# Expert weights in 2 MB pieces of 16 KB runs for pairs of experts, and a next-to-last piece in two parts

## The chip, the cores and the metric

The kernel runs on one core of a Trainium2 chip. The metric is the device time of one execution in microseconds. Before the change the median of three runs is 1400.31 us (1399.62 to 1402.27).

## The reference, cut to what matters

One layer for 256 tokens of width 1024, in float32. A mixer with four branches (RWKV7, HGRN2, mLSTM, RG-LRU) is followed by a layer norm, a mixture of 32 experts with the best four for each token, a gated projection called PLE, and a second layer norm:

```python
mix = merged @ w_out[layer]                      # merged: the four gated branches
x = _layernorm(DEEPNORM_ALPHA * x + mix, ln1_g[layer], ln1_b[layer], dt)
moe_out = moe(x.reshape(bsz * seq, D_MODEL), router_w[layer], ...)
ple = jax.nn.sigmoid(x @ ple_gate_w[layer]) * (p[layer] @ ple_proj_w[layer])
x = _layernorm(DEEPNORM_ALPHA * x + moe_out + ple, ln2_g[layer], ln2_b[layer], dt)
```

An expert takes its tokens through a product of 1024 x 2048 (`w_gu`, a gate half and an up half of 1024 columns each), a clamped SwiGLU, and a product of 1024 x 1024 (`w_dn`). The weights of 32 experts are 403 MB in float32, and each is used once.

## The kernel before, in words

Phase 1 (to about 435 us) computes the four branches, the merge, the first layer norm and the router. Its products are made of three passes each (lines 378 to 380) on operands that ACT and DVE split into a high and a low part (lines 373 and 374). Phase 2 is the expert stage. Experts go in 16 pairs; the first expert of a pair uses partitions 0 to 63 of a PSUM bank, the second 64 to 127.

All weights come through one list, `stream`, filled by `want` in the order of use. Before, an entry is one 1 MB piece of one expert: 512 rows by 512 columns, laid out in HBM as 128 runs of 8,192 bytes, one for each partition (`chunks`, line 2117). The two experts of a pair alternate in the list. For one pair, `want_up` (line 1392) lists four column blocks x two row halves x two experts, and `want_down` (line 1399) two x two x two. For two of the pairs (`PLE`) it also lists half of `w_pg` in two pieces, and half of `w_pp` (512 KB).

`pump` (line 311) walks the list as far as there are buffers, and issues each transfer on SP's queue. There are two kinds of buffers. The 14 slots (`NSLOT`, line 202) hold 8 KB on each partition. The rest is the `Arena` (line 128), from which all other tiles come as well; its allocator likes to keep whole blocks of 2,048 float columns free (`B`), and `ar.blocks()` counts those. `st["keep"]` is a reserve of buffers that the stream leaves for other tiles once `st["slots"]` is 0, which is the case in the expert stage. `drop` (line 368) gives a piece's buffer back; from there the next transfer follows by the semaphores: SP waits for the last reader of the buffer, and for the landing that had the same semaphore before (eight of them go round).

`prod` (line 1697) makes the products of one block: for each of the four 128-row steps of a piece one product for each expert of the pair (line 1705), 16 products for two pieces; behind the fourth step it drops both pieces and calls `pump`. `up` makes gate, up and SwiGLU, `turn` (line 1793) transposes the result, `down` makes the second product, and `combine` (line 1727) adds a half of a pair's result into the output by eight products with a 0/1 matrix. `gather` (lines 1660 to 1680) collects the tokens of two pairs, once for every second pair, and `down_bias` (1739, 1745) comes once. `ple` (line 1862) makes 32 products with both halves of `w_pg` (line 1868), dropping each half after its 16, then 8 with `w_pp` (line 1878). In the last pair, `ending` (line 1756) takes over for the second column block: with the first row half it makes 32 products for two 256-column halves (line 1762), combines the other column block, and then takes the second row half, whose transfers come in six parts of 1 KB runs (line 326). A chain on DVE (lines 2060 to 2067) makes the layer norm and four transfers write the output.

The order of the work on PE, ACT, DVE and POOL is the order in which the program is written out; the lag between `up` and `down` is one pair. Which buffers a tile gets is settled when the program is built, and with that the waits on their earlier users.

Of the kernel before, what the change touches and what calls it, by code (L numbers as in the profile page):

```python
# [20 lines left out]
T = 256  # L21
# [106 lines left out]
class Arena:  # L128


    G, B = 32, 2048 // 32

    def __init__(self, t, cols):
        self.t, self.n = t, cols // self.G
        self.used = np.zeros(self.n, bool)
        self.freed = np.zeros(self.n, np.int64)
        self.now, self.live, self.peak, self.tight, self.low = 1, {}, 0, False, False

    def get(self, shape, dt=F32):
# [9 lines left out]
        if self.tight:  # L149
# [3 lines left out]
            else:  # L153
                whole = np.repeat(~self.used[:self.n // B * B].reshape(-1, B).any(axis=1), B)
                whole = np.append(whole, np.zeros(self.n - len(whole), bool))
                w = w + np.where(np.lib.stride_tricks.sliding_window_view(whole, g).any(axis=1), 1 << 40, 0)
        if self.low:
            w = np.where(w < 1 << 60, w >> 40 << 40, w) + np.arange(len(w))
# [43 lines left out]
NSLOT = 14  # L202
# [9 lines left out]
def hybrid_kernel(ctx: ExitStack, tc: tile.TileContext, xT, x, w_in, pc_d, rows_d, cn_d, lv_d, wa2, g2, lrub, w_br,  # L212
# [91 lines left out]
    st = {"next": 0, "out": 0, "ahead": 4, "slots": 1, "keep": 3}  # L304
    LATE = "br2_3"
    tails = [("dn", e, 512, 1) for e in (NE - 2, NE - 1)]

    def want(key, src, shape):
        stream.append((key, src, shape))

    def pump():
        while st["next"] < len(stream):
# [3 lines left out]
            if key in tails:  # L316
                if len(sl.idle) < len(tails):
                    break
                for key, _, shape in stream[st["next"]:]:
                    t = sl.get(F32)  # L320
                    place[key] = (sl.free, t)
                    ready[key] = in_slot(t, shape)
                for cc, k, n in ((0, 0, 4), (256, 0, 2), (256, 2, 2)):
                    for key, src, _ in stream[st["next"]:]:
                        src = src.rearrange("p (k c) -> p k c", k=4)
                        SY.dma_start(ready[key][:, k:k + n, cc:cc + 256], src[:, k:k + n, cc:cc + 256])
                st["next"] = len(stream)
                break
            spare = ar.blocks() if ar.tight else 0
            if st["slots"] == 0 and spare + len(sl.idle) <= st["keep"]:  # L330
                break
            if len(sl.idle) > st["slots"]:
                t = sl.get(F32)
                place[key] = (sl.free, t)
                ready[key] = in_slot(t, shape)
            elif spare > (st["keep"] if st["slots"] else 0):
                ready[key] = al(shape)
                place[key] = (fr, ready[key])
            elif late and st["out"] < 2:
                release(late.pop(0)[1])  # L340
                continue
            else:
                break
            if st["next"] == 0:
# [15 lines left out]
    def drop(key):  # L360
        f, t = place.pop(key)
        f(t)
        del ready[key]
        st["out"] -= 1
# [225 lines left out]
    def rwkv():  # L590
# [56 lines left out]
        BK_t = sl.get(F32)  # L647
        BK = in_slot(BK_t, [128, 4, 512]).rearrange("p c (n i s) -> p c n i s", n=4, i=2)
        AR_t = sl.get(F32)
        AR = in_slot(AR_t, [128, 4, 512]).rearrange("p c (n i s) -> p c n i s", n=4, i=2)  # L650
# [77 lines left out]
        BKt_t = sl.get(F32)  # L728
        BKt = in_slot(BKt_t, [128, 4, 512])
# [35 lines left out]
        sl.free(BK_t)  # L765
# [144 lines left out]
        sl.free(AR_t)  # L910
        sl.free(BKt_t)
# [480 lines left out]
    def want_up(i):  # L1392
        for half in ((0, 0), (1, 0), (0, 1), (1, 1)):
            c0 = half[0] * D + half[1] * 512
            for k in range(2):
                for e in (2 * i, 2 * i + 1):
                    want(("gu", e, c0, k), w_gu[e, c0 // 512, k], [128, 4, 512])

    def want_down(i):
        for j in range(2):  # L1400
            for k in range(2):
                for e in (2 * i, 2 * i + 1):
                    want(("dn", e, j * 512, k), w_dn[e, j, k], [128, 4, 512])
        if i in PLE:
            j = PLE.index(i)
            for k in range(2):
                want(("pg", 0, j * 512, k), w_pg[j, k], [128, 4, 512])
# [10 lines left out]
    pump()  # L1418
    lz["pc"] = fetch(pc_d, [128, NPC])
    lz["half"] = al([128, 1])  # L1420
    G.memset(lz["half"], -0.5)
    lz["wa2"] = fetch(wa2, [128, W])
    st["ahead"] = 3
    pump()
    lz["cn"] = fetch(cn_d[:, 0:KEPT], [128, KEPT])
    lz["cn2"] = fetch(cn_d[:, KEPT:NCN], [128, NCN - KEPT])
# [65 lines left out]
    y_t = sl.get(F32R)  # L1492
# [206 lines left out]
    def prod(p, se, ex, lhs, kind, c0, b0, ks):  # L1699

        if ks[0] == 0 and b0 is not None:
            biased(p, se, c0, b0)
        for k in ks:
            for a in range(2):
                PE.matmul(p[64 * a:64 * a + 64], lhs(a, k), chunk(kind, ex[a], c0, k // 4)[:, k % 4],  # L1705
                          start=b0 is None and k == 0, stop=k == KT - 1)
# [11 lines left out]
    def new_rest():  # L1718
        ybuf.append(ybuf.pop(0))
# [35 lines left out]
    def ending(ex, lhs, ow):  # L1755
# [4 lines left out]
        def down(h, k, s):  # L1760
            for a in range(2):
                PE.matmul(ps[h][64 * a:64 * a + 64, 0:256], lhs(a, k), ready["dn", ex[a], 512, s][:, k % 4, part[h]],
                          start=k == 0, stop=k == KT - 1)

        for h in range(2):
            for k in LO:
                down(h, k, 0)
        combine(*rest.pop())
# [29 lines left out]
    def up(i):  # L1798
# [32 lines left out]
        if i == 0:  # L1831
            st["keep"] = 5
# [30 lines left out]
    def ple(j):  # L1863
        cc = slice(j * 512, j * 512 + 512)
        pp = [bank(), bank()]
        for k in range(KT):
            for t in range(2):
                PE.matmul(pp[t], xT1[:, k, t * 128:t * 128 + 128], chunk("pg", 0, j * 512, k // 4)[:, k % 4],
                          start=k == 0, stop=k == KT - 1)
            if k % 4 == 3:  # L1870
                drop(("pg", 0, j * 512, k // 4))
                pump()
# [24 lines left out]
    def overflow(e, ec, blk_no):  # L1897
# [33 lines left out]
        def dyn(w, c):  # L1931
            ts = [al([128, 4, 512]) for i in range(2)]
            for i in range(2):
                SY.dma_start(flat(ts[i]), w[bass.ds(e, 1), c, i].rearrange("o p c -> p (o c)"))
# [219 lines left out]
```

## Time and profile before

| | |
|---|---|
| median of three runs | 1400.31 us |
| the profiled execution | 1402.92 us |
| its span in the trace | 1400.5 us |
| PE busy | 1294.5 us (92%) |
| DVE, ACT, POOL busy | 504.4, 330.6, 187.6 us |
| moved by DMA | 474.84 MB, 339 GB/s over the span |
| granted TensorE clock, mean | 0.986 of full speed |

Busy PE is a sum over two phases with different limits, so it is read by stretches: the weight list is in full flow from about 448 us on. Times in the rows below are us from the span's start.

### The profile page before, as it was taken

How to read it: one execution, taken by the hardware profiler on the slowest of the kernel's cores; microseconds unless marked ns; L12 is line 12 of the kernel's file. 1: busy time of each engine (PE TensorE's matmuls, PEld its weight loads, DVE VectorE, ACT ScalarE, POOL GpSimd, SP SyncE). 2: the span in 40 equal slices, each digit the busy share in tenths (PEclk: the TensorE clock that was granted, in tenths of full speed). 3: DMA queues.
4: the chain of work that ended last, by engine and by line, in shares of the span. 5: the costliest groups of instructions: out<-in, count | busy, mean ns of one | idle time of the engine just before them, and what ended most of it. 6: DMA issues, size and time to landing. Idle time of an engine off the chain costs nothing. (4 is left out here: it accounts for less than half of the span.)

```text
span 1400.5 us, 17423 instructions
## 1 busy us (share of the span) xinstructions
PE 1294.5 (92%) x7269; PEld 717.8 (51%) x7269; DVE 504.4 (36%) x715; ACT 330.6 (24%) x499; POOL 187.6 (13%) x197
## 2 busy tenths in 40 slices
PE   8988899999999998999889999989988898898985
PEld 8977879999994342333224333423433332342332
DVE  5887876686674122121121212201121211121114
ACT  6765654665433010010001000100100100010000
POOL 0578944413100000000000000000000000000000
PEclk9999999999999999999999999999999999999998
DMA  9413244458566999999999999999999999999995
GB/s 350 156 42 136 91 137 138 148 184 333 201 247 275 422 421 410 421 421 422 421 421 420 417 420 421 421 421 421 421 421 421 420 422 421 422 421 421 422 421 188
DMA packets 80151, 474.84 MB, mean 339 GB/s; under 512 B 14114, under 2 KB 20898, under 8 KB 24388
## 3 DMA queue, kind: packets, MB, share of 16 engines
q1 hardware_dynamic: 80068, 473.68, 83.7%
q8 instruction: 59, 0.97, 0.3%
q14 instruction: 24, 0.20, 0.0%
HBM read 472.07 MB, written 1.57 MB: 338 GB/s over the span
## 5 line engine op out<-in xcount | busy, mean ns | idle before, releaser
L1705 PE MATMUL bank<-slot,arena 128*64 128x512 f32 x2856 | 712.1, 600 | 58.1 <-DMA slot<-in_w_dn 32.1
L1705 PEld LDWEIGHTS bank<-slot,arena 128*64 128x64 f32 x2856 | 224.4, 137 | 460.7 <-issue 326.2
L378 PE MATMUL bank<-slot,slot 128*128 128x256 f32 (+2 forms) x800 | 243.9, 305 | 5.0 <-ACT slot L407 5.0
L379 PE MATMUL bank<-slot,slot 128*128 128x256 f32 (+2 forms) x800 | 239.6, 300 | 2.1 <-DVE slot L374 2.1
L380 PE MATMUL bank<-slot,slot 128*128 128x256 f32 (+2 forms) x800 | 239.7, 300 | 2.0 <-DVE slot L374 2.0
L378 PEld LDWEIGHTS bank<-slot,slot 128*128 128x128 f32 (+1 forms) x800 | 155.1, 194 | 11.7 <-ACT slot L407 5.0
L380 PEld LDWEIGHTS bank<-slot,slot 128*128 128x128 f32 (+1 forms) x800 | 155.1, 194 | 7.0 <-DVE slot L374 2.8
L379 PEld LDWEIGHTS bank<-slot,slot 128*128 128x128 f32 (+1 forms) x800 | 155.2, 194 | 6.2 <-DVE slot L374 2.5
L374 DVE TENSOR_TENSOR slot<-slot,slot 128x1024 fp32r<-128x1024 f32 (+1 forms) x89 | 123.8, 1399 | 47.8 <-ACT slot L373 47.6
L1695 DVE TENSOR_SCALAR arena<-bank 128x512 f32<-128x512 f32 x32 | 22.1, 692 | 236.9 <-PE bank L1705 230.1
L373 ACT CAST slot<-slot 128x1024 fp32r<-128x1024 f32 (+1 forms) x99 | 101.4, 1040 | 13.3 <-DVE slot L374 5.5
L1694 ACT ACTIVATE arena<-arena 128x512 f32<-128x512 f32 x32 | 20.2, 631 | 347.2 <-DVE arena L1693 347.2
L1716 DVE SCALAR_TENSOR_TENSOR slot<-bank,arena,slot 128x512 fp32r<-128x512 f32 (+1 forms) x33 | 24.2, 735 | 209.4 <-ACT slot L1715 209.1
L1581 POOL CAST se<-arena 128x128 fp32r<-128x128 f32 x16 | 5.0, 322 | 670.0 <-PE bank L1588 622.6
L1728 DVE TENSOR_TENSOR arena<-arena,bank 128x512 f32<-128x512 f32 (+1 forms) x66 | 40.1, 667 | 131.0 <-PE bank L1727 131.0
L1715 ACT ACTIVATE slot<-bank,arena 128x512 fp32r<-128x512 f32 (+1 forms) x33 | 22.3, 676 | 264.8 <-PE bank L1705 255.1
L1705 PE MATMUL bank<-arena 128*64 128x512 f32 x184 | 73.3, 599 | 5.4 <-DMA arena<-in_w_dn 2.7
L1693 DVE TENSOR_SCALAR arena<-bank 128x512 f32<-128x512 f32 x32 | 22.1, 689 | 120.6 <-PE bank L1705 120.6
L540 POOL TENSOR_TENSOR arena<-arena 128x4 f32<-128x4 f32 (+2 forms) x10 | 9.8, 990 | 354.7 <-DVE arena L2061 293.2
L1541 ACT ACTIVATE arena<-bank,arena 128x256 f32<-128x256 f32 x36 | 20.1, 566 | 114.1 <-DVE arena L1543 114.1
L1705 PEld LDWEIGHTS bank<-arena 128*64 128x64 f32 x184 | 21.0, 138 | 38.1 <-issue 26.8
L1794 ACT COPY arena<-bank 128x512 f32<-128x512 f32 x32 | 17.2, 590 | 92.3 <-PE bank L1793 92.3
(373 smaller groups left out, 1074.4 us busy)
## 6 DMA issues: line engine op xcount, KB each, us to landing
slot<-in_w_gu SPq DMA_DIRECT2D x237, 1024.0 KB, 18.6
slot<-in_w_dn SPq DMA_DIRECT2D x122, 1024.0 KB, 19.8
slot<-in_w_in SPq DMA_DIRECT2D x38, 1024.0 KB, 4.9
arena<-in_w_gu SPq DMA_DIRECT2D x19, 1024.0 KB, 16.0
slot<-in_w_br SPq DMA_DIRECT2D x7, 1024.0 KB, 4.9
slot<-in_w_pg SPq DMA_DIRECT2D x4, 1024.0 KB, 16.0
arena<-in_w_dn SPq DMA_DIRECT2D x4, 1024.0 KB, 19.9
arena<-in_w_in SPq DMA_DIRECT2D x3, 1024.0 KB, 7.7
```

Of the source, the lines that this page charges most:

```text
L373: S.copy(hi, src)
L374: (lo_eng or V).tensor_sub(lo, src, hi)
L378: PE.matmul(o, a[0], b[0], start=first, stop=False)
L379: PE.matmul(o, a[0], b[1], start=False, stop=False)
L380: PE.matmul(o, a[1], b[0], start=False, stop=last)
L1693: V.tensor_scalar_min(g_, pg[0], 7.0)
L1694: S.activation(s_, g_, AF.Sigmoid, scale=1.702)
L1695: V.tensor_scalar(u_, pg[1], -7.0, 7.0, op0=ALU.max, op1=ALU.min)
L1705: PE.matmul(p[64 * a:64 * a + 64], lhs(a, k), chunk(kind, ex[a], c0, k // 4)[:, k % 4], start=b0 is None and k == 0, stop=k == KT - 1)
L1715: S.activation(y[:, 0], p, AF.Copy, scale=w)
L1716: V.scalar_tensor_tensor(y[:, 1], p, w, y[:, 0], op0=ALU.mult, op1=ALU.subtract)
L1728: V.tensor_add(moe[t][:, o:o + n], moe[t][:, o:o + n], p[:, 0:n])
```

## The change

A piece becomes 2 MB: the same 512 rows by 512 columns of both experts of a pair, laid out side by side, so that each partition has one run of 16,384 bytes. The list has one entry where it had two, and `w_pg` one where it had two. A piece takes either one arena block, whose size grows from 2,048 to 4,096 columns (one DMA), or two slots (two DMAs with 8 KB runs). Slots go from 14 to 11, and the room of the three goes to the arena; three tiles of RWKV move from slots to the arena, and phase 1's own pieces look in the arena first (`one`). The reserve `keep` goes from 5 to 6 in the expert stage. `ple` gives its piece back after all 32 products. The next-to-last piece (`LAST[0]`) comes in four transfers of two row steps each, with 4 KB runs, and `ending` makes the products of its first two row steps for both column halves, then the other block's combination, then those of the last two.

```diff
-    G, B = 32, 2048 // 32
+    G, B = 32, 4096 // 32
...
-NSLOT = 14
+NSLOT = 11
...
+    TAIL = ("dn", NE // 2 - 1, 512, 1)
+    LAST = ("dn", NE // 2 - 1, 512, 0), TAIL
...
+    def two(key, src):
+
+        spare, idle = ar.blocks(), len(sl.idle) - st["hold"]
+        if st["slots"] == 0 and 2 * spare + idle <= st["keep"] + 1:
+            return False
+        if spare > (0 if st["slots"] == 0 else st["keep"] // 2):
+            t = al([128, 2, 4, 512])
+            placed(key, [t], fr)
+            ready[key] = t[:, 0], t[:, 1]
+            if key not in LAST:
+                SY.dma_start(t.rearrange("p e k c -> p (e k c)"), src.rearrange("p e f -> p (e f)"))
+            return True
+        if idle >= st["slots"] + 2:
+            ts = [sl.get(F32) for a in range(2)]
+            placed(key, ts, sl.free)
+            ready[key] = [in_slot(t, [128, 4, 512]) for t in ts]
+            if key not in LAST:
+                for a in range(2):
+                    SY.dma_start(ts[a][:, 0:2048], src[:, a])
+            return True
+        return False
...
+            if key == LAST[0]:
+                for k in (0, 2):
+                    for a in range(2):
+                        w = src[:, a].rearrange("p (k c) -> p k c", k=4)
+                        SY.dma_start(ready[key][a][:, k:k + 2], w[:, k:k + 2])
...
             if k % 4 == 3:
-                for a in range(2):
-                    drop((kind, ex[a], c0, k // 4))
-                    pump()
+                drop((kind, i, c0, k // 4))
+                pump()
...
-        for h in range(2):
-            for k in LO:
-                down(h, k, 0)
-        combine(*rest.pop())
+        for k0 in (0, 2):
+            for h in range(2):
+                for k in (k0, k0 + 1):
+                    down(h, k, 0)
+            if k0 == 0:
+                combine(*rest.pop())
...
         if i == 0:
-            st["keep"] = 5
+            st["keep"] = 6
...
-            if k % 4 == 3:
-                drop(("pg", 0, j * 512, k // 4))
-                pump()
+        drop(("pg", 0, j * 512))
+        pump()
```

What that makes of the order on the engines, at three places. First, SP's queue in the middle of the expert stage, around the first `w_pg`; names are the buffer and the tensor, then partitions x elements. Before:

```order
L356 DMA slot_5584<-in_w_dn 128x2048
L356 DMA slot_5586<-in_w_dn 128x2048
L356 DMA slot_5597<-in_w_dn 128x2048
L356 DMA slot_5599<-in_w_dn 128x2048
L356 DMA slot_5609<-in_w_pg 128x2048
L356 DMA slot_5611<-in_w_pg 128x2048
L356 DMA slot_5627<-in_w_pp 128x1024
L356 DMA slot_5629<-in_w_gu 128x2048
L356 DMA slot_5702<-in_w_gu 128x2048
L356 DMA slot_5704<-in_w_gu 128x2048
```

Now (x8 stands for eight such transfers in a row):

```order
L349 DMA arena<-in_w_gu 128x4096 x8
L349 DMA arena<-in_w_dn 128x4096 x4
L349 DMA arena<-in_w_pg 128x4096
L395 DMA slot_5414<-in_w_pp 128x1024
L349 DMA arena<-in_w_gu 128x4096 x8
L349 DMA arena<-in_w_dn 128x4096 x4
L349 DMA arena<-in_w_pg 128x4096
```

Two rows with 8 KB runs in slots became one with 16 KB runs in the arena, and the two of `w_pg` became one; `w_pp` stays in a slot.

Second, the end of the same queue (in the row of six, the last two are the last pair's first column block). Before:

```order
L356 DMA slot_8017<-in_w_dn 128x2048
L356 DMA slot_8019<-in_w_dn 128x2048
L326 DMA slot_8032<-in_w_dn 128x4x256
L326 DMA slot_8033<-in_w_dn 128x4x256
L326 DMA slot_8032<-in_w_dn 128x2x256
L326 DMA slot_8033<-in_w_dn 128x2x256
L326 DMA slot_8032<-in_w_dn 128x2x256
L326 DMA slot_8033<-in_w_dn 128x2x256
```

Now:

```order
L349 DMA arena<-in_w_gu 128x4096 x8
L349 DMA arena<-in_w_dn 128x4096 x6
L375 DMA arena<-in_w_dn 128x1024 x4
L380 DMA arena<-in_w_dn 128x4x256 x2
L380 DMA arena<-in_w_dn 128x2x256 x4
L2113 DMA out<-arena 128x512 x4
```

The next-to-last 2 MB, two transfers before, are the four of 128x1024; the six of the last 2 MB are the same.

Third, PE in the ending: the last products of line 1762 with the first row half, the combination (1727), and the first with the second row half. Before:

```order
L1762 MATMUL bank_8086<-slot_8017,arena 64x256
L1762 MATMUL bank_8086<-slot_8019,arena 64x256
L1762 MATMUL bank_8086<-slot_8017,arena 64x256
L1762 MATMUL bank_8086<-slot_8019,arena 64x256
L1727 MATMUL bank_8103<-slot_4251,slot_4174 128x512 x2
L1727 MATMUL bank_8107<-slot_4251,slot_4174 128x512 x2
L1762 MATMUL bank_8085<-slot_8032,arena 64x256
L1762 MATMUL bank_8085<-slot_8033,arena 64x256
L1762 MATMUL bank_8085<-slot_8032,arena 64x256
L1762 MATMUL bank_8085<-slot_8033,arena 64x256
```

Now, from the last products ahead of the ending on (lines 1744, 1804 and 1769 are what 1705, 1762 and 1727 were):

```order
L1744 MATMUL bank_7488<-arena 64x512 x8
L1804 MATMUL bank_7515<-arena 64x256 x4
L1804 MATMUL bank_7516<-arena 64x256 x4
L1769 MATMUL bank_7525<-slot_4678,slot_4135 128x512 x2
L1769 MATMUL bank_7529<-slot_4678,slot_4135 128x512 x2
L1804 MATMUL bank_7515<-arena 64x256 x4
L1804 MATMUL bank_7516<-arena 64x256 x4
L1804 MATMUL bank_7515<-arena 64x256 x8
L1804 MATMUL bank_7516<-arena 64x256 x4
```

The combination stood behind all 32 products with that row half; now 16 of them, in two rows of 4 x 2 halves, stand ahead of it and as many behind.

## Rows read from the trace of the kernel before

**Rows 1.** The page, 40 slices of the span (35 us each): GB/s moved; and the DMA queues: packets, MB, share of the 16 engines' span.

```profile
GB/s 350 156 42 136 91 137 138 148 184 333 201 247 275 422 421 410 421 421 422 421 421 420 417 420 421 421 421 421 421 421 421 420 422 421 422 421 421 422 421 188
...
q1 hardware_dynamic: 80068, 473.68, 83.7%
q8 instruction: 59, 0.97, 0.3%
```

**Rows 2.** Busy time of the engines in stretches of the expert stage (us; x instructions), then granted TensorE clock, DMA share and GB/s.

```profile
448.00:500.00 52.00, 52.00 (x240) 17.28 (x238) 10.14 (x17) 2.97 (x5) 0.83 (x3) 1.00 1.01 422
...
1000.00:1050.00 50.00, 46.04 (x196) 16.93 (x194) 9.24 (x14) 3.51 (x6) 0.29 (x1) 1.00 1.01 422
...
1300.00:1350.00 50.00, 46.02 (x195) 16.77 (x192) 9.24 (x14) 3.71 (x6) 0.00 (x0) 1.00 1.01 421
```

**Rows 3.** The waits of PE and of SP's queue over the whole span: engine, line, what it waited for, us in total, times, longest.

```profile
PE bank L1705 <- DMA slot<-in_w_dn: 32.1, 26, 1.3
PE bank L1705 <- DMA slot<-in_w_gu: 25.9, 21, 1.3
...
SPq L356 <- DMA slot<-in_w_gu: 291.0, 152, 3.3
SPq L356 <- PE bank L1705: 287.5, 156, 17.8
```

**Rows 4.** PE's timeline in the middle of the expert stage: start, us, line, count, and in brackets the idle time before it with its releaser.

```profile
1047.30 3.65 PE L1705 MATMUL bank<-slot,arena 128*64 128x512 f32 x16 [1.33 <-DMA slot<-in_w_dn]
1052.27 3.65 PE L1705 MATMUL bank<-slot,arena 128*64 128x512 f32 x16 [1.31 <-DMA slot<-in_w_dn]
```

**Rows 5.** The page's DMA issues: count, KB each, median us from issue to landing.

```profile
slot<-in_w_gu SPq DMA_DIRECT2D x237, 1024.0 KB, 18.6
slot<-in_w_dn SPq DMA_DIRECT2D x122, 1024.0 KB, 19.8
slot<-in_w_in SPq DMA_DIRECT2D x38, 1024.0 KB, 4.9
```

**Rows 6.** PE's timeline from the first expert product, and at the end of that stretch.

```profile
434.45 3.87 PE L1705 MATMUL bank<-arena 128*64 128x512 f32 x16
...
549.78 3.65 PE L1705 MATMUL bank<-slot,arena 128*64 128x512 f32 x16 [1.31 <-DMA slot<-in_w_gu]
```

**Rows 7.** Stretches of 2 us at the end of the weight stream, columns as in rows 2.

```profile
1376.00:1378.00 2.00, 1.11 (x10) 0.77 (x12) 0.75 (x1) 0.22 (x1) 0.00 (x0) 1.00 1.04 348
1378.00:1380.00 2.00, 2.00 (x21) 1.32 (x18) 0.00 (x0) 0.00 (x0) 0.00 (x0) 1.00 0.60 201
```

**Rows 8.** PE's timeline around the down bias (lines 1739 and 1745) and a gather (lines 1660 to 1680).

```profile
613.00 0.39 PE L1739 MATMUL bank<-arena 128*32 128x128 f32 x2
...
619.02 5.44 PE L1705 MATMUL bank<-slot,arena 128*64 128x512 f32 x16
624.40 4.09 PE L1660 MATMUL bank<-oh,slot 128*128 128x256 f32 x32
...
629.60 10.51 PE L1705 MATMUL bank<-slot,arena 128*64 128x512 f32 x48
```

**Rows 9.** PE's timeline around the first PLE (lines 1868 and 1878).

```profile
743.33 0.41 PE L1680 MATMUL bank<-arena,oh 128*64 128x1 f32 x8
...
754.02 14.00 PE L1868 MATMUL bank<-slot,arena 128*128 128x512 f32 x32
...
767.86 3.60 PE L1878 MATMUL bank<-slot,arena 128*128 128x512 f32 x8
...
771.81 3.65 PE L1705 MATMUL bank<-slot,arena 128*64 128x512 f32 x16
```

**Rows 10.** Stretches of 5 us inside that PLE, columns as in rows 2.

```profile
755.00:760.00 5.00, 5.00 (x13) 2.26 (x12) 0.69 (x1) 0.00 (x0) 0.00 (x0) 1.00 1.01 419
760.00:765.00 5.00, 5.00 (x13) 2.24 (x12) 0.00 (x0) 0.00 (x0) 0.00 (x0) 1.00 1.02 424
```

**Rows 11.** The timelines of ACT and DVE at two places of phase 1.

```profile
73.39 0.21 ACT L938 ACTIVATE arena<-arena 128x4 f32<-128x4 f32 x1 [5.17 <-POOL arena L937]
...
75.39 0.36 ACT L921 COPY arena<-bank 128x256 f32<-128x256 f32 x1
...
75.52 2.58 DVE L374 TENSOR_TENSOR slot<-slot,slot 128x1024 fp32r<-128x1024 f32 x1 [1.71 <-ACT slot L373]
...
132.77 1.09 ACT L927 ACTIVATE arena<-bank 128x512 f32<-128x512 f32 x2
135.06 0.59 ACT L737 COPY slot<-bank 128x512 f32<-128x512 f32 x1 [1.20 <-PE bank L736]
...
141.28 0.63 ACT L993 ACTIVATE arena<-arena 128x512 f32<-128x512 f32 x1 [1.93 <-POOL arena L997]
...
137.57 1.32 DVE L374 TENSOR_TENSOR slot<-slot,slot 128x1024 fp32r<-128x1024 f32 x1
```

**Rows 12.** PE's timeline in the ending (line 1762 its products, 1727 the combinations).

```profile
1376.89 3.67 PE L1762 MATMUL bank<-slot,arena 128*64 128x256 f32 x30 [1.24 <-DMA slot<-in_w_dn]
...
1380.49 1.20 PE L1727 MATMUL bank<-slot,slot 128*128 128x512 f32 x4
...
1381.61 2.81 PE L1762 MATMUL bank<-slot,arena 128*64 128x256 f32 x24
...
1385.21 1.08 PE L1762 MATMUL bank<-slot,arena 128*64 128x256 f32 x8
```

More of the change, by code (lines that the diff above doesn't have):

```diff
@@ L315, in pump @@
                 break
[L316 to L322, printed above, removed]
-                for cc, k, n in ((0, 0, 4), (256, 0, 2), (256, 2, 2)):
[L324 to L344, printed above, removed]
+            if not (two(key, src) if shape is None else one(key, src, shape)):
+                if late and st["out"] < 2:
+                    release(late.pop(0)[1])
+                    continue
+                break
+            if key == LAST[0]:
[3 more added lines that the diff above has]
+                        SY.dma_start(ready[key][a][:, k:k + 2], w[:, k:k + 2])
+            elif key == TAIL:
+                for cc, k, n in ((0, 0, 4), (256, 0, 2), (256, 2, 2)):
+                    for a in range(2):
+                        w = src[:, a].rearrange("p (k c) -> p k c", k=4)
+                        SY.dma_start(ready[key][a][:, k:k + n, cc:cc + 256], w[:, k:k + n, cc:cc + 256])
+            elif shape is None:
+                pass
+            elif st["next"] == 0:
                 src = src.rearrange("p (k c) -> p k c", k=KT)
@@ L360, in drop @@
     def drop(key):
-        f, t = place.pop(key)
-        f(t)
+        back, tiles = place.pop(key)
+        for t in tiles:
+            back(t)
         del ready[key]
@@ L764, in rwkv @@
             yield
-        sl.free(BK_t)
+        fr(BK_t)
         fr(vp)
@@ L1395, in want_up @@
             for k in range(2):
-                for e in (2 * i, 2 * i + 1):
-                    want(("gu", e, c0, k), w_gu[e, c0 // 512, k], [128, 4, 512])
+                want(("gu", i, c0, k), w_gu[i, c0 // 512, k], None)
     def want_down(i):
@@ L1401, in want_down @@
             for k in range(2):
-                for e in (2 * i, 2 * i + 1):
-                    want(("dn", e, j * 512, k), w_dn[e, j, k], [128, 4, 512])
+                want(("dn", i, j * 512, k), w_dn[i, j, k], None)
         if i in PLE:
             j = PLE.index(i)
-            for k in range(2):
-                want(("pg", 0, j * 512, k), w_pg[j, k], [128, 4, 512])
+            want(("pg", 0, j * 512), w_pg[j], None)
             want(("pp", 0, j * 512, 0), w_pp[j], [128, 2, 512])
@@ L1718, in new_rest @@
     def new_rest():
+        if not ybuf:
+            st["hold"] = 0
+            y_t = sl.get(F32R)
+            ybuf.extend(in_slot(y_t, [128, 4, 512])[:, 2 * i:2 * i + 2] for i in range(2))
         ybuf.append(ybuf.pop(0))
@@ L1978, in overflows @@
             G.memset(ec, 0.0)
-            with tc.For_i(0, NE) as e:
-                for blk_no in range(2):
-                    overflow(e, ec, blk_no)
-                V.tensor_scalar_add(ec, ec, 1.0)
+            with tc.For_i(0, NE // 2) as e2:
+                for a in range(2):
+                    for blk_no in range(2):
+                        overflow(e2, a, ec, blk_no)
+                    V.tensor_scalar_add(ec, ec, 1.0)
             for j in range(2):
@@ L1987, in overflows @@
         done_with(*ob)
-    ybuf = [in_slot(y_t, [128, 4, 512])[:, 2 * i:2 * i + 2] for i in range(2)]
+    ybuf = []
+    st["hold"] = 1
     first = gather(0)
```

65 lines of the change are left out of this document (45 added, 20 removed).

## The prediction

> **What bounds it now.** I read the page's 40 slices first: from slice 13 on the DMA engines move about 421 GB/s, to the last slice but one [rows 1]. Windows of 50 us from 448 on then show a DMA share of 1.01 at 421 or 422 GB/s, while PE has 46 busy in the later ones [rows 2]: the expert stage runs at the pace of the weight stream. PE waits for that stream again and again (58 us ahead of products from w_gu and w_dn, [rows 3]); on its timeline one 2 MB step of 16 products starts every 4.97 us (1047.30, 1052.27), although its products take only 3.65 [rows 4]. SP, which issues every transfer, waits 287.5 us for PE to give buffers back and 291.0 for landings of w_gu [rows 3]: transfers queue deep, each landing 18.6 to 19.8 us after its issue [rows 5], so PE can come late by about that much before a DMA engine idles. That depth is what the change alters most.
>
> One stretch is different. From 434.45 to 549.78 PE works through what was loaded ahead; its first wait for a weight piece is the one of 1.31 us before 549.78 [rows 6]. Until then PE sets the time, and the stream after that.
>
> The profiled execution took 1402.92 us, 2.6 above the median 1400.31; its span, 1400.5, is the trace. The sum below is a difference read from that execution, and I add it to the median. A measurement of this kernel can tell some 0.2%, 2.8 us, from no change.
>
> **The term that gains: longer runs.** Bytes per second at full share depend on the run. At the end only 1 KB runs are left: 348 GB/s at a share of 1.04, then 201 at 0.60, so 335 GB/s per full share [rows 7]; 16 engines x 1024 bytes / 335 GB/s = 48.9 ns a run. With 8 KB runs it is 421.5 GB/s at 1.01: 311 ns a run, 314 ns of busy share. A line a + b x KB through both gives a = (8 x 48.9 - 314)/7 = 11 ns that every run costs apart from its bytes; without correcting for shares above 1 (348 GB/s, 47.1 ns; 311 ns) it is 9.4. I take **10 ns**. A 2 MB piece is 8 runs of 16 KB on each engine in place of 16 of 8 KB: 8 x 10 = 80 ns off 4.96 us. From 549.78 to about 1372, before the short runs begin, there are (1372 - 549.8)/4.96 = 166 pieces: **-13.3 us**. Ahead of 549.78 a faster stream gains nothing by itself, as PE sets the time there. No row of before shows a weight run of 16 KB. The nearest from below is the 8 KB run (no gain); from above the line with 11 ns (-14.6). The fetches of instructions are 16 KB packets too (59, 0.97 MB), at 0.3% of 16 engines, 67 us, 1.1 us each [rows 1], nearly twice what two 8 KB runs take; they are another queue's, few and scattered, and wait among weight packets, so I give them no weight.
>
> The Trainium skill speaks of this ("DMA: Bandwidth & Descriptors", section "Why small descriptors are slow"): a fixed overhead of about 3 cycles for each packet. With the 850 MHz of the same page that is an estimate of 3.5 ns; by it the term would be -4.7 us in place of -13.3 and the sum +5.3 in place of -3.3. The rows on 1 KB runs show about 10 ns, so they differ, but no row tests it on long runs.
>
> **The term that loses: depth.** Before, SP holds nine or ten 1 MB buffers in flight or in use in steady state. In the change the order on SP shows every steady piece going to an arena block of 4,096 columns; none goes to the seven idle slots, since `two` stops at `2 * spare + idle <= keep + 1`, which with no spare block, seven idle slots and keep 6 reads 7 <= 7. Following the allocator through the program, **four** 2 MB buffers are left: one under PE's products, three for the stream. Three hold 3 x 4.88 = 14.6 us of it. From that go the 3.4 us in which PE reads the fourth, and what passes between a buffer's release and bytes flowing again: a lone 1 MB transfer lands 4.9 us after its issue [rows 5], 2.5 of them bytes, so 2.4. PE may be late by 14.6 - 3.4 - 2.4 = **8.8 us** before the engines idle (before: about 18). Whatever idles there is lost, since the stream is the bound. What makes PE late:
> - A gather: 624.40 to 629.60, 5.2 us [rows 8]. Under 8.8: nothing. The one at 624 follows the down bias (613.00 to 619.02, 6.0) with one piece between that makes up 4.96 - 3.55 = 1.4: 6.0 - 1.4 + 5.2 = 9.8, so **+1.0**.
> - PLE, twice. Its 32 products take 13.84 us (754.02 to 767.86) and 8 more 3.5; the next piece starts at 771.81 [rows 9]. Before, the first 1 MB of w_pg was free after half the products; now both halves are one buffer, given back at the end. Measured against a normal reading of 3.44, that buffer is 10.4 late: 1.6 over. The next is free at 771.81 + 3.44, that is 21.2 after the start instead of 8.3: 12.9 late, less the 1.6 already lost, 2.5 over. The 512 KB of w_pp, in its own slot, keep the engines at work for 1.2 of that. 1.6 + 2.5 - 1.2 = 2.9 each. The first PLE comes three pieces after a gather (10.51 us from 743.58) and inherits 5.7 - 3 x 1.4 = 1.5. Together **+7.3**. Today these 18 us are wholly covered: 419 and 424 GB/s through 755 to 765 [rows 10]. If PLE's products hide as now the term is 0; if only two buffers stand behind it, it is 4.9 a time more, +17.
> - Start of the stage: the queue is 16 MB ahead instead of 15 and then shrinks to 8. Engines will idle somewhere in 480 to 510, but PE has its data there, and it sets the time: 0, less than 2 if idle engines let PE catch up early.
>
> **Phase 1.** Fewer slots and other places for buffers make new waits on reuse. By the built program's waits, the copy of line 921 at 75.39 must now wait for DVE's split of line 374 (75.52 + 2.58 = 78.10), and the activation of line 927 at 133.3 for the split that ends 137.57 + 1.32 = 138.89 [rows 11]: 2.3 and 5.5 us on ACT. Just before the first ACT idles 5.17 us, so PE is not waiting on ACT there; I count 0. Behind the second ACT idles 1.20 and 1.93 us, which take up part of it; PE's branch products queue behind the rest: **+2.4**. Ends: 0, and 7.8 if nothing is taken up. PE sets the time until 549.78, so all of it counts.
>
> **The end.** The next-to-last piece comes in 4 KB runs: 512 runs, 32 an engine instead of 16, +16 x 10 ns; with one larger handoff, **+0.3**. PE idles 1.24 us before 1376.89, then works on to 1386.3 without a wait [rows 12]: 32 products, combination, 32 products. Now half of the 32 and the combination (4 products, 1.1 us) can run before the piece's second half has landed. At most the 1.24 is filled: **-1.0**, ends 0 and -1.24. The DVE chain behind it, 9 us, stays.
>
> **Sum:** -13.3 + 1.0 + 7.3 + 2.4 + 0.3 - 1.0 = **-3.3 us**, 1400.3 - 3.3 = **1397.0**.
>
> **Rivals.**
> 1. *The depth is never used up.* PE's lateness at PLE and in phase 1 is absorbed, DMA stays at a share of 1.01: -13.3 - 1.0 + 0.3 = -14, 1386. For it: PE idles about 1.3 us before most pieces, and no window falls today. Against: 13.84 us on one buffer against 8.8. Chance 0.2.
> 2. *Long runs save less than short ones say.* The place is the stream from 550 to 1372; the price of a run beyond its bytes decides. The losses add up to +10.0; 166 x 8 runs save as much at 7.5 ns each. Under that the change is slower: at 5 ns, half of what the short runs show, +3.4 (1403.7), at none +10 (1410). For it: the line is drawn from 1 KB runs, and at 8 KB 16 such costs are 3% of a piece, within what a share printed as 1.01 can hide. Against: both corrections give 9 or more. Chance 0.22. The page of the Trainium skill named above lies on this side, with its 3.5.
> 3. *The two cancel.* One more stall, for instance each of the later gathers by 0.4, or 9 ns: within 2.8 of no change, 1398 to 1403. Chance 0.23.
>
> My forecast, a gain of 2.8 to 10 (1390 to 1397.5), has the remaining 0.35; with rival 1 faster comes to 0.55, within 0.2% 0.23, slower 0.22. The range takes in rival 1 and most of rival 2: 1386 to 1406.
>
> **What the changed profile would show.** The run length: 50-us windows without a stall at 427 or 428 GB/s (right), or 421 to 422 (rival 2). The depth: a DMA share under 1 in the 20 us behind the start of each PLE, some 3 to 4 us lost, and again near 625; a share of 1.01 throughout would be rival 1. Landing of w_gu pieces: 14 to 20 us after issue. Phase 1: the first expert products about 2.4 us later than 434.45. The end: products on both sides of the combination, with a last weight wait between them and no wait of over a microsecond ahead of the first half. I am wrong if idle time shows at ordinary gathers, or if the windows rise by other than 5 to 7 GB/s.

## The result and the profile after

The change takes 1409.39 us (median of four, 1407.96 to 1410.18) against 1400.33: slower by 0.6%, ratio 1.006 with a 95% interval of 1.0045 to 1.0075. The prediction was 1397.0 with a range of 1386 to 1406, so the sign was wrong and the time lies outside. The profiled execution took 1409.63 us, its span is 1407.8, 7.3 above that of before.

Stretches of 50 us of the changed kernel, columns as in [rows 2], and below them three of the same stretches of the kernel before:

```profile
600.00:650.00 50.00, 44.47 (x201) 17.69 (x200) 9.93 (x17) 5.13 (x10) 0.29 (x1) 0.90 0.90 368
750.00:800.00 50.00, 49.69 (x189) 19.34 (x187) 9.33 (x14) 4.27 (x7) 0.00 (x0) 1.00 0.95 381
800.00:850.00 50.00, 43.86 (x158) 15.71 (x155) 6.17 (x9) 3.20 (x5) 0.29 (x1) 1.00 0.96 403
850.00:900.00 50.00, 48.75 (x251) 20.25 (x249) 12.26 (x22) 5.75 (x10) 0.29 (x1) 1.00 0.97 399
1000.00:1050.00 50.00, 46.49 (x236) 19.30 (x238) 11.53 (x20) 6.43 (x11) 0.00 (x0) 1.00 1.01 427
1300.00:1350.00 50.00, 45.31 (x188) 15.17 (x186) 7.26 (x11) 6.05 (x10) 0.00 (x0) 0.97 1.01 428
```

```profile
600.00:650.00 50.00, 48.22 (x220) 19.37 (x217) 10.42 (x18) 6.19 (x11) 0.29 (x1) 0.93 1.01 421
750.00:800.00 50.00, 50.00 (x190) 19.20 (x188) 9.26 (x14) 4.22 (x7) 0.29 (x1) 1.00 1.01 418
850.00:900.00 50.00, 50.00 (x256) 20.48 (x252) 10.81 (x19) 5.87 (x11) 0.29 (x1) 1.00 1.01 421
```

Where nothing stalls, the stream moves 426 to 429 GB/s, mostly 427 or 428, instead of 421 or 422. In four windows it doesn't: (428 - 368)/428 x 50 = 7.0 us lost in the first, then 5.5, 2.9 and 3.4. The first holds the gather behind the down bias, the second the first PLE, the last two the second PLE. In all other windows from 550 to 1350 the share is 1.00 or 1.01, also with the gathers at 744 and from 1000 on.

PE's timeline around the second PLE (line 1912 was 1868, 1921 was 1878, 1744 was 1705), to be held against [rows 9]:

```profile
831.44 13.97 PE L1912 MATMUL bank<-arena 128*128 128x512 f32 x32 [1.34 <-DMA arena<-in_w_pg]
845.25 3.60 PE L1921 MATMUL bank<-slot,arena 128*128 128x512 f32 x8
848.78 0.50 PE L1626 MATMUL bank<-slot,se 64*128 64x512 f32 x1
849.21 3.65 PE L1744 MATMUL bank<-arena 128*64 128x512 f32 x16
852.79 1.09 PE L1837 MATMUL bank<-arena 128*128 128x128 f32 x8
853.82 3.65 PE L1744 MATMUL bank<-arena 128*64 128x512 f32 x16
857.40 2.11 PE L1769 MATMUL bank<-slot,slot 128*128 128x512 f32 x8
859.44 0.49 PE L1626 MATMUL bank<-slot,se 64*128 64x512 f32 x1
859.86 7.09 PE L1744 MATMUL bank<-arena 128*64 128x512 f32 x32
```

A buffer comes free when the piece on it is read: 13.8 us after the start, then 21.4, 26.0 and 32.0 (859.86 + 3.55). On time would be 3.6, 8.5, 13.4 and 18.3. PE is 10.2, 12.9, 12.6 and 13.7 us late: the turn (1.09), the combination (2.11) and the biases behind PLE eat up what the pieces make good. The engines' time there:

```profile
844.00:848.00 4.00, 4.00 (x11) 1.85 (x10) 0.72 (x2) 0.60 (x1) 0.00 (x0) 1.00 0.51 123
848.00:852.00 4.00, 4.00 (x17) 1.26 (x18) 2.04 (x3) 0.60 (x1) 0.00 (x0) 1.00 1.01 434
852.00:856.00 4.00, 4.00 (x23) 1.63 (x20) 0.00 (x0) 1.07 (x2) 0.00 (x0) 1.00 0.52 139
...
860.00:866.00 6.00, 6.00 (x30) 2.01 (x30) 1.25 (x3) 0.63 (x1) 0.00 (x0) 1.00 0.97 369
```

By (428 - 123)/428 x 4, 2.9 us are lost while the first buffer comes free, then 2.7 at the second and 0.8 at the fourth, 6.4 in all. Up to each of them the loss is the lateness less 7.3: 10.2 - 2.9, 12.9 - 5.6, 13.7 - 6.4.

The down bias and the gather behind it (lines 1787, 1698), against [rows 8], and below them the window with the granted clock, the third column from the end:

```profile
611.08 3.65 PE L1744 MATMUL bank<-arena 128*64 128x512 f32 x16 [1.24 <-DMA arena<-in_w_gu]
...
616.89 0.36 ACT L1782 COPY arena<-bank 32x256 f32<-32x256 f32 x1 [10.54 <-DVE arena L1735]
617.30 6.80 PE L1787 MATMUL bank<-arena 32*128 32x512 f32 x8 [2.24 <-ACT arena L1782]
624.03 5.59 PE L1744 MATMUL bank<-arena,slot 128*64 128x512 f32 x16
629.55 4.10 PE L1698 MATMUL bank<-oh,slot 128*128 128x256 f32 x32
...
634.76 10.51 PE L1744 MATMUL bank<-arena,slot 128*64 128x512 f32 x48
```

```profile
620.00:625.00 5.00, 5.00 (x9) 1.35 (x9) 2.24 (x4) 0.00 (x0) 0.00 (x0) 0.50 1.01 429
```

The bias products before (line 1745 was what 1787 is now) and a window with their clock:

```profile
613.84 5.25 PE L1745 MATMUL bank<-arena 32*128 32x512 f32 x8 [0.45 <-ACT arena L1740]
```

```profile
615.00:620.00 5.00, 5.00 (x10) 1.40 (x10) 2.96 (x6) 0.00 (x0) 0.00 (x0) 0.58 1.01 413
```

The copy that the bias products need now waits for DVE, and PE stands still for 2.24 us (0.45 before). The granted clock then is at 0.50 (1.2 GHz). It fell in the kernel before too, but only from 616 on, when part of the eight products was done; now it is down for nearly all of them, and they take 6.80 us instead of 5.25. Bias and handoff take 614.7 to 624.0, 9.4 us instead of 6.0, and the piece behind them takes 5.5 us, as it did before (5.4), where a piece takes 3.6 at full clock. Counted as at PLE, from 611.08 on, the buffers behind the bias come free 10.0 and 13.8 us late.

At the start of the stage the stream has gaps too. The window from 450 to 550 before, in the change, and in e1_keep2, which has two buffers more (below):

```profile
450.00:550.00 100.00, 98.69 (x470) 36.45 (x468) 20.50 (x35) 9.43 (x16) 1.12 (x4) 1.00 1.01 418
```

```profile
450.00:550.00 100.00, 98.03 (x472) 36.32 (x470) 20.50 (x35) 9.52 (x17) 1.12 (x4) 1.00 0.96 397
```

```profile
450.00:550.00 100.00, 100.00 (x484) 37.24 (x482) 20.51 (x35) 9.40 (x16) 1.12 (x4) 1.00 1.00 413
```

PE first waits for a weight piece at 542.56 in the change, 549.78 before and 552.39 in e1. Against the kernel before that costs nothing: the third turn begins 143.5 us behind the first expert product, 143.8 before. But with five to seven buffers (e1, e2, e7, e9, e10) it begins 139.8 to 140.5 behind it.

### The profile page after: what moved, and what is told of

Same layout as the page of the kernel before. It is cut to its first block, busy times and chain, and to the rows that moved or that the text cites. A ratio compares the mean times of both kernels' runs of the same rounds, so it can differ in the third digit from the quotient of the medians.

```text
span 1407.8 us, 17065 instructions
## 1 busy us (share of the span) xinstructions
PE 1261.6 (90%) x7269; PEld 694.5 (49%) x7269; DVE 504.1 (36%) x715; ACT 328.9 (23%) x499; POOL 185.0 (13%) x197
## 5 line engine op out<-in xcount | busy, mean ns | idle before, releaser
L1744 PE MATMUL bank<-arena 128*64 128x512 f32 x2816 | 640.6, 600 | 90.0 <-DMA arena<-in_w_gu 53.5
L1744 PEld LDWEIGHTS bank<-arena 128*64 128x64 f32 x2816 | 194.3, 137 | 481.3 <-issue 331.7
L418 PEld LDWEIGHTS bank<-slot,slot 128*128 128x128 f32 (+1 forms) x800 | 154.5, 193 | 14.1 <-ACT slot L447 5.2
L414 DVE TENSOR_TENSOR slot<-arena,slot 128x1024 fp32r<-128x1024 f32 (+1 forms) x69 | 96.5, 1411 | 23.6 <-ACT slot L413 23.4
L413 ACT CAST slot<-arena 128x1024 fp32r<-128x1024 f32 (+1 forms) x75 | 75.8, 1035 | 3.7 <-DMA arena<-in_w_in 2.9
L414 DVE TENSOR_TENSOR slot<-slot,slot 128x1024 fp32r<-128x1024 f32 x30 | 40.2, 1340 | 33.1 <-ACT slot L413 33.1
L1769 PE MATMUL bank<-slot,slot 128*128 128x512 f32 (+1 forms) x132 | 35.1, 403 | 0.7 <-ACTq L2020 0.6
L413 ACT CAST slot<-slot 128x1024 fp32r<-128x1024 f32 x34 | 35.3, 1043 | 1.2 <-issue 1.1
```

The lines of the kernel that those rows point to most:

```text
L413: S.copy(hi, src)
L414: (lo_eng or V).tensor_sub(lo, src, hi)
L418: PE.matmul(o, a[0], b[0], start=first, stop=False)
L1744: PE.matmul(p[64 * a:64 * a + 64], lhs(a, k), chunk(kind, i, c0, k // 4)[a][:, k % 4], start=b0 is None and k == 0, stop=k == KT - 1)
L1769: PE.matmul(p[:, 0:n], ow[0][:, half, t], y[:, i], start=i == 0, stop=i == 1)
```

## The experiments

For comparing programs, phase 1 is best taken off, because it varied (below). The columns are the time from the first expert product to the end of the span (966.1 before, 970.9 in the change), and the median with the ratio to before.

| run | expert stage, us | median, us | ratio (95%) |
|---|---|---|---|
| e1_keep2 | 952.6 | 1395.23 | 0.9969 (0.9952 to 0.9987) |
| e2_keep0 | 954.7 | 1397.59 | 0.9976 (0.9957 to 0.9994) |
| e3_run8 | 980.6 | 1421.86 | 1.0150 (1.0121 to 1.0179) |
| e4_pgslots | 968.8 | 1409.76 | 1.0066 (1.0040 to 1.0092) |
| e5_before_keep7 | 966.2 | 1401.21 | 1.0005 (0.9996 to 1.0014) |
| e6_before_tail | 964.8 | 1399.25 | 0.9989 (0.9980 to 0.9998) |
| e7_slots9_keep2 | 952.0 | 1389.39 | 0.9919 (0.9905 to 0.9932) |
| e8_slots14_keep2 | 963.5 | 1398.58 | 0.9983 (0.9974 to 0.9992) |
| e9_slots9_keep4 | 956.0 | 1389.52 | 0.9918 (0.9905 to 0.9932) |
| e10_keep4 | 953.9 | 1397.43 | 0.9970 (0.9956 to 0.9984) |
| e11_before_keep9 | 967.3 | 1401.09 | 1.0000 (0.9991 to 1.0010) |
| e12_short_ple | 959.2 | 1400.96 | 0.9997 (0.9982 to 1.0012) |
| e13_before_last7 | 976.4 | 1409.92 | 1.0078 (1.0055 to 1.0100) |
| e14_before_last9 | 999.2 | 1435.82 | 1.0255 (1.0238 to 1.0272) |

**More buffers for the same pieces** (e1, e2, e10).

```diff
-            st["keep"] = 6
+            st["keep"] = 2     # e2: 0, e10: 4
```

> The change with one number altered: in the expert stage the reserve keep is 2 instead of 6, so that a piece may also go to a pair of idle slots. Buffers of 2 MB out at a time go from 4 to 6; 78 of the 194 pieces then come in slot pairs with 8 KB runs, the other 116 keep 16 KB runs. Theory (depth): the DMA engines idle about 5 us at 625-650, 5 at 770-800 and 6 at 840-870 only because four buffers let PE be no more than about 9 us late; six allow about 18, so nearly all of these 16 us come back, less 78 x 80 ns = 6 us of run gain: 1409.4 - 16 + 6 = about 1399, DMA share 1.01 in those three stretches. Rival (unit): a 2 MB unit is released and landed as a whole, which costs whatever the number of buffers; then the share stays at 0.90 to 0.97 there and the time rises by the lost run gain to about 1415.

> As e1_keep2 with keep 0: seven buffers of 2 MB, 92 of the 194 pieces in slot pairs with 8 KB runs. Theory (depth): the stalls are gone already with six, so the seventh brings nothing and 14 more pieces lose 80 ns each: about 1 us above e1_keep2, 1400. If the lateness to be covered is larger than 18 us, it is below e1_keep2. Rival (unit): about 1416.

> The change with keep 4 and 11 slots: four blocks and one slot pair, five buffers of 2 MB. Between the change (four) and e1_keep2 (six). Theory (depth decides, the fifth buffer is what is missing): windows at 600-650, 750-800, 800-850 and 850-900 back to 422 or more; the expert stage like e1_keep2, about 1395. Rival (the loss falls evenly with depth): halfway, about 1402.

Windows of e1_keep2 and the slowest of e10_keep4:

```profile
600.00:650.00 50.00, 45.69 (x204) 18.42 (x204) 9.93 (x17) 6.17 (x11) 0.29 (x1) 0.90 1.00 424
750.00:800.00 50.00, 49.55 (x186) 19.28 (x188) 9.27 (x14) 4.21 (x7) 0.29 (x1) 1.00 1.01 424
850.00:900.00 50.00, 50.00 (x258) 20.63 (x256) 12.25 (x21) 6.44 (x11) 0.29 (x1) 1.00 1.01 427
```

```profile
750.00:800.00 50.00, 50.00 (x191) 19.38 (x189) 9.32 (x14) 4.27 (x7) 0.00 (x0) 1.00 1.01 414
```

The stalls are gone with six buffers, and all but gone with five; the expert stage falls by 18.3 and 17.0 us and a seventh brings nothing. I had expected 10 for e1; some 4 of the rest lie ahead of 580 us, at the start of the stage. The 2 MB unit is not the trouble, the number is: PE is as late as in the change (from the start of the second PLE to the third piece of w_gu behind it pass 28.4 us in both), and the stream runs on.

**Run length** (e3): two transfers of 8 KB runs into the same block.

```diff
-                SY.dma_start(t.rearrange("p e k c -> p (e k c)"), src.rearrange("p e f -> p (e f)"))
+                for a in range(2):
+                    SY.dma_start(t[:, a].rearrange("p k c -> p (k c)"), src[:, a])
```

> The change with its arena pieces brought by two transfers of 1 MB with 8 KB runs each, into the same 2 MB block, same buffers, same releases. Theory (16 KB runs save some 75 to 80 ns a piece, depth costs the rest): windows without a stall fall from 428 to 421 GB/s, stalls stay where they are, a little shorter since a slower stream takes longer to drain the buffers: plus 10 to 13 us, 1420. Rival (run length is worth nothing, the 428 come from fewer or larger transfers): 428 GB/s stay and the time is 1409.

Two of its windows:

```profile
850.00:900.00 50.00, 49.91 (x240) 20.76 (x240) 13.50 (x23) 6.26 (x11) 0.29 (x1) 1.00 0.93 371
1000.00:1050.00 50.00, 47.35 (x235) 20.96 (x233) 11.55 (x20) 5.81 (x10) 0.00 (x0) 1.00 1.01 421
```

421 again, with the stalls where they were: the median is 12.5 us above the change, the expert stage 9.7. The runs do save what was forecast: 2 MB take 4.976 us at 421.5 GB/s and 4.900 at 428, 76 ns for eight runs, 9.5 ns a run. e3 doubles the number of transfers as well, so by itself it does not part the two. The records of single packets in the trace of e1 do, where both lengths come in one stream: from 910 to 1350 us a packet of 16 KB takes 616 ns on average and one of 8 KB 314. That is 2 x 314 - 616 = 12 ns within the packets, whatever passes between transfers.

**Who keeps PE late, and who holds the buffer** (e4, e12). e4 puts w_pg in two idle slots and gives each half back after its 16 products; e12 leaves out 24 of the 32 products (the text on record says 28 and reckons with 24).

```diff
+        if key[0] == "pg":                                   # e4, in two()
+            ts = [sl.get(F32) for a in range(2)]
...
-        for k in range(KT):                                  # e12, in ple()
+        for k in (0, KT - 1):
```

> The change with w_pg alone in two of the idle slots (two 1 MB transfers with 8 KB runs), each half given back after its 16 products; everything else as in the change. Theory (depth, at PLE): w_pg no longer takes one of the four blocks for 13.8 us, PE may be 4.9 us later there; of the 5 + 6 us lost behind the two PLEs about 9 come back: 1400. Rival (PLE's loss comes from the work of PE behind it, turns and combinations that keep PE late, whoever holds w_pg): less than 3 come back, 1407 or more. The stall of 5 us at 625-650 must stay in both.

> The change with 28 of the 32 products with w_pg left out of each PLE (two of its eight row steps remain); all transfers as in the change. Theory (PE's time in PLE makes it late): 24 x 0.43 = 10.3 us less at each, under the 8.8 that four buffers allow, so the 5 and 6 us of idle engines near 775 and 850 vanish: 1398 to 1400; the stall at 625-650 stays. Rival (the shape of PLE's transfers, 2 MB and then 512 KB of 4 KB runs, makes the gap): share and time as in the change.

A window of e4_pgslots, then one of e12_short_ple:

```profile
850.00:900.00 50.00, 48.95 (x248) 20.17 (x249) 13.51 (x23) 6.34 (x11) 0.29 (x1) 1.00 0.94 386
```

```profile
850.00:900.00 50.00, 45.30 (x235) 17.94 (x231) 9.16 (x16) 5.65 (x11) 0.30 (x1) 1.00 1.01 428
```

The two halves of w_pg, freed early, were worth only 2 us: back in slots that the rule keeps idle, they brought no transfer forward. SP waits for no product with w_pg in e4, and yet some 5 us are lost at each PLE (384 GB/s from 750 to 800, 386 from 850 to 900). With PE's time gone the stall is gone, with the same transfers; the one near 625 stays (371 GB/s in 600 to 650). e12 also frees w_pg earlier, but by e4 that is worth 2 us. So PE's whole lateness around PLE sets the stall, as e4's rival had it.

**What had made the old kernel safe** (e5, e11, then e13, e14). The number out in the kernel before was cut by its reserve:

```diff
-            st["keep"] = 5
+            st["keep"] = 7                     # e11: 9
...
-        i = self.idle.pop(0)                   # e13 (7) and e14 (9) only
+        i = self.idle.pop(-1 if self.last else 0)
```

> The kernel before (1 MB pieces, 8 KB runs, 14 slots) with one number altered: keep 7 instead of 5 in the expert stage, so that 8 (or 7) pieces of 1 MB are out at a time instead of 10 (or 9): about the 8 MB that the change has. Theory (depth in bytes): the same three stretches (down bias and gather near 620, both PLEs) now stall here too, 4 to 6 us each, and no other: plus 12 to 15 us, about 1414. Rival (unit of 2 MB): pieces of 1 MB with as many bytes out do not stall: within 3 us of 1400.

> The kernel before with keep 9: 6 (or 5) pieces of 1 MB out at a time, after 8 (7) cost nothing. Counting releases and stream by the profile's durations: behind a PLE's start 3.5 MB are left, 8.7 us, halves come back 7 and 13.8 us later, so some 4 us idle for each; down bias and gather idle 2.5 + 3.7. Theory (what PE's lateness needs is more than what is left in the buffers): plus 12 to 16 us, 1413 to 1416, in the same three stretches. Rival (1 MB units do not stall whatever their number): within 3 us of 1400.

Both were misses for my theory: with 8 and even 6 MB counted as out, the share stays at 1.01 everywhere, and landing at 18.1 and 18.4 us for w_gu. Idle slots are taken in turn, the one given back first is used first, so a transfer waits for a reader of long ago: the reserve goes round and is depth, though the count leaves it out. To test that, the last one given back is taken first:

> The kernel before with keep 7 as in e5_before_keep7, and in the expert stage the slot given back last is taken first (before: the one given back first). Only then do 8 (7) MB out bound the stream: with the queue of idle slots going round, a transfer waits for a reader of long ago, and the reserve serves as depth. Theory (that is why e5 and e11 did not stall; 8 MB in 1 MB pieces nearly suffice): landing falls from 18 to about 16 us, about 1 us idle behind the down bias, 1400 to 1403. Rival (order of the slots does not matter): landing stays at 18 us and the time at 1401.

> As e13_before_last7 with keep 9: 6 (5) MB really bound the stream. Theory: what was expected of e11 now happens, in the same three stretches as in the change: some 6 us idle at 620-640 and 4 for each PLE, 1412 to 1417; landing about 11 us. Rival (1 MB pieces do not stall, or the order does not matter): 1401.

The line of w_gu among the DMA issues, and a window, of e13 and then of e14:

```profile
slot<-in_w_gu SPq DMA_DIRECT2D x247, 1024.0 KB, 14.1
...
750.00:800.00 50.00, 50.00 (x190) 19.99 (x187) 9.27 (x14) 4.22 (x7) 0.30 (x1) 1.00 0.97 385
```

```profile
slot<-in_w_gu SPq DMA_DIRECT2D x247, 1024.0 KB, 9.7
...
750.00:800.00 50.00, 50.00 (x219) 22.18 (x217) 9.68 (x16) 7.01 (x12) 0.00 (x0) 1.00 0.87 347
```

Nothing but the order of equal slots differs from e5 and e11, the landing falls from 18.1 to 14.1 and from 18.4 to 9.7 us, and the expert stage is 10 and 32 us longer, with stalls at the PLEs and, in e14, near 625 and 1300 too. Both came out slower than I expected (1400 to 1403, 1412 to 1417). In e13 the engines idle at the PLEs and not behind the down bias (420 GB/s from 600 to 650), where I had expected it. So the direction holds, and the places in e14 alone; my counting of when engines run dry is too kind by some microseconds for each stall.

**The ending alone** (e6: the kernel before with the change's ending and the four transfers).

> The kernel before with the ending of the change alone: the next-to-last 2 MB in four transfers of 4 KB runs by halves of its row steps, half of its products ahead of the combination and half behind. Theory: fills the 1.24 us in which PE waits at 1376.89 before: minus 1.0 to 1.3, read as the time from the last weight byte to the end in the trace, as 0.1% lies under what the times tell. Rival: nothing, since PE is late anyway when those pieces land.

Its PE in the ending (line 1777 was 1762, 1742 was 1727):

```profile
1374.04 2.17 PE L1777 MATMUL bank<-slot,arena 128*64 128x256 f32 x16
1376.14 1.20 PE L1742 MATMUL bank<-slot,slot 128*128 128x512 f32 x4
1377.27 4.54 PE L1777 MATMUL bank<-slot,arena 128*64 128x256 f32 x40
```

The wait of 1.24 us in [rows 12] is gone; expert stage -1.3, median -1.3 against the runs of before beside it.

**Slots and phase 1** (e7, e8, e9).

```diff
-NSLOT = 11
+NSLOT = 9       # e7 with keep 2, e9 with keep 4; e8: 14 with keep 2
```

> The change with keep 2 as in e1_keep2 and 9 slots instead of 11, the room of two slots going to the arena as a fifth block of 4,096 columns for the stream: six 2 MB buffers out as in e1_keep2, but only some 30 pieces in slot pairs with 8 KB runs instead of 78. Theory (depth and run length add): no stalls, and 48 more pieces save 80 ns: 4 us below e1_keep2, 1391, if phase 1 is not slower with fewer slots. Rival (fewer slots delay phase 1 more): the expert stage alone gains 4 us, and the first expert product comes later by as much or more.

> The change with keep 2 and 14 slots as before; the arena loses the three slots' room, most pieces come in slot pairs with 8 KB runs. Theory (phase 1 is later in the change for want of slots): the first expert product comes as early as in the kernel before, 2 to 6 us earlier than in the change; the expert stage without stalls at 422 to 424 GB/s, so about 1399. Rival (the new places of tiles, not the number of slots, delay phase 1): the first expert product is as late as in the change.

> As e7_slots9_keep2 with keep 4: the five arena blocks alone are out at a time (six late in the stage), and every steady piece has 16 KB runs. Theory: 33 more pieces save 80 ns each, -2.6 us against e7_slots9_keep2, and five blocks still cover the two PLEs and the gather behind the down bias, whose lateness with four was 1 to 6 us over: at most 1 us of stall each. 1387 to 1389. Rival (six are needed): 5 us and more are lost in the three stretches, 1392 or more.

e7 and e9 beat the kernel before by 11 us and the change by 20. Windows 750 to 800 of e7 and then of e9:

```profile
750.00:800.00 50.00, 50.00 (x188) 19.37 (x190) 9.27 (x14) 3.53 (x6) 0.29 (x1) 1.00 1.01 426
```

```profile
750.00:800.00 50.00, 49.69 (x188) 19.16 (x186) 9.27 (x14) 4.21 (x7) 0.30 (x1) 1.00 0.99 406
```

Five blocks are not quite enough (e9 loses (428 - 406)/428 x 50 = 2.6 us here, 2.3 at 600 to 650 and 2.2 from 800 to 900, where I had expected at most 1 each), six are. The expert stage of e7 is only 0.6 below that of e1 where I expected 4, although fewer pieces come in 8 KB runs; why, no run shows. Its median is 5.8 lower, as its runs scatter less (1388.8 to 1390.2 against 1390.3 to 1399.7 in e1). On phase 1 my theory on slots holds for e8 (first expert product at 433.31, as in the kernel before), but not for e7 and e9: with still fewer slots it is at 435.64 and 437.06, within 0.2 us of the change or earlier.

**Phase 1 of the change** varies. Seven programs with its 11 slots had the first expert product anywhere from 435.85 to 443.82 (change 436.87, e2 443.82), against 430.70 to 434.45 in those built on the kernel before. PE's waits in the change at the start of this:

```profile
144.63 1.12 PE L1043 MATMUL bank<-arena 128*64 128x64 f32 x16 [4.33 <-DVE arena L1038]
161.00 0.39 PE L418 MATMUL bank<-slot,slot 128*128 128x256 f32 x1 [2.30 <-ACT slot L413]
```

Behind the second wait the clock stays at 1.00 in the change and falls in e2, whose windows are these:

```profile
160.00:165.00 5.00, 2.60 (x12) 2.40 (x13) 3.34 (x6) 3.41 (x6) 4.33 (x9) 0.70 0.62 211
165.00:170.00 5.00, 5.00 (x20) 4.11 (x19) 4.86 (x8) 3.54 (x6) 4.17 (x7) 0.50 0.00 0
```

The two executions are 0.6 us apart at this stall, 6.1 at a later wait (before 247.56 in the change) and 7.0 at the first expert product, which is 2.4 us later than before in the one and 9.4 in the other. The times of programs with 11 slots scatter by up to 11 us (e2), and the clock goes with it: in e1 the four runs up to 1393 us have a mean granted clock of 0.985 to 0.987, the four above 1398 have 0.980 to 0.982.

## Why the prediction was wrong

The balance of the profiled executions: runs -12.6 (166 x 76 ns; predicted -13.3); stalls 7.0 + 5.5 + 2.9 + 3.4 = +18.8 (predicted 1.0 + 7.3 = 8.3); first expert product 436.87 against 434.45, +2.4 (predicted +2.4); ending -1.3, taken from e6 (predicted -1.0 + 0.3). Sum +7.3, and the span is 7.3 longer. The medians differ by 9.1; the profiled execution of before was 2.6 above its median, and in which stage the others are shorter no trace shows.

- **Longer runs: right.** 9.5 ns a run where I took 10. The estimate of 3.5 ns that I had worked out from the Trainium skill's page "DMA: Bandwidth & Descriptors" (section "Why small descriptors are slow") is too low: at 8 and 16 KB a run costs 9.5 ns. Rival 2, which rested on cheaper runs, fails, though the time it gave (1403.7 to 1410) was nearest.
- **Depth: the step that failed; the mechanism right, its price less than half** (8.3 predicted, 18.8 measured). Both sizes in it were off.
  - *How late PE is.* At PLE I counted up to the second buffer (12.9) and took the third as made good. PE's turn, combinations and biases behind PLE keep it there: 13.7 at the fourth, and e12 shows that it is this time and e4 that it is not the holding of w_pg. At the down bias I counted 9.8, and PE is 13.8 late: I carried 6.0 us over from before, and a new wait made it 9.4, 1.8 more of standing still and 1.5 more in the products at the lower clock; and the piece behind it, which was to make up 1.4, took 5.5 us. That it does so stood in [rows 8], 619.02 to 624.40.
  - *How late it may be.* I had 8.8 us. By what was lost it is 13.7 - 6.4 = 7.3 at the second PLE, 13.7 - 5.5 = 8.2 at the first and 13.8 - 7.0 = 6.8 behind the down bias. From the release of w_pg at 845.25 to full flow at 848 pass some 2.7 us, more than the 2.4 that I allowed for both ends of a transfer, and no relief by the 1.2 us of w_pp is to be seen; more than that no run shows of why it is less. So the PLEs cost 5.5 and 6.3 instead of 4.4 and 2.9, the down bias 7.0 instead of 1.0. The 1.5 that I let the first PLE inherit is not there: PE waited 0.31 us for w_pg ahead of it, and the 5.7 in that working stands in no row (a gather takes 5.2).
- **The start of the stage: 0 as predicted, in part by luck.** "Ahead of 549.78 a faster stream gains nothing" is wrong where the buffers suffice: with five to seven of them the third turn came 3 to 4 us earlier. In the change the gaps in the stream took that gain away.
- **"Before: about 18."** The margin of before was real (PE is late by as much at its PLEs, and the share stays at 1.01), but I put it down to the nine or ten pieces counted as out. e5, e11, e13 and e14 show that the reserve went round as depth; the change turned that into seven slots that no steady piece uses. That is its actual loss.
- **Phase 1: +2.4, right by luck.** The wait I named did come (PE 4.33 before 144.63, 2.63 in the kernel before), but at 154.69 PE was only 0.3 later than before. Then another stall (2.30 at 161.00) made it 3.8, by 195 it was 1.6, a third wait (1.46 before 247.56, for ACT) made it 3.7, and 2.4 were left at the first expert product.
- **The end: right**, and confirmed by e6. The wait for weights that I expected between the halves does not show.

What stays open is the scatter of phase 1. The trace shows what the stall at 161.00 waits for (last section), but no run takes that away, and none shows why the clock falls behind it in one execution and not in another. Why PE may be late by less behind the down bias than at the first PLE was not tested either.

## What to carry to other kernels

Price a deeper or shallower queue by the longest stretch in which the consumer does other work, catch-up included, not by its single steps; and ask which buffers ever rotate, not how many are counted as out. A gain of 1.5% in the stream is lost to a few stalls of 5 to 7 us: e7 keeps it by having six 2 MB buffers.

## What the runs showed of the hardware

A short DVE instruction took almost six times as long beside a long one on POOL. The same sum of two 4x256 tiles before, in the change, and POOL at that time in the change:

```profile
152.75 0.41 DVE L1097 TENSOR_TENSOR arena<-arena,slot 4x256 f32<-4x256 f32 x1
```

```profile
155.65 2.37 DVE L1135 TENSOR_TENSOR arena<-arena 4x256 f32<-4x256 f32 x1
...
155.30 2.44 POOL L1070 TENSOR_TENSOR arena<-arena 128x1024 f32<-128x1024 f32 x1 [0.50 <-ACT arena L1069]
```

Before, the sum ran ahead of the long one on POOL (155.00 to 157.40); the split of line 374, which ran beside that one from 156.20, took 2.28 us, and 1.2 to 1.4 at its four other places between 144 and 165 us. The Trainium skill ("GPSIMD Engine Reference", section "1. Specifications") lists the SBUF interfaces as shared between the two engines, with contention where a DVE instruction has two SBUF inputs, which agrees; no run here tests it. It precedes the stall at 161.00: DVE's row of short instructions ends 2 us later by it, and ACT's cast waits behind that row. The second surprise is the price of the clock: the PE stall of 2.30 us at 161 was followed by 10 us at 0.50 in e2 (165 to 175) and by none in the change, whose programs are the same up to that point.
